# Later norm broadcast, later transposes of branches B and C, later cross-attention scores in a two-layer decoder trunk

## Chip, cores and metric

The kernel runs on one core of one Trainium2 chip. The metric is the time of one execution on the device in microseconds (us), and of several executions the median. "Faster" and "slower" compare the changed kernel with the one before.

## What is computed

Two layers of a causal decoder trunk on 512 tokens of width 1024, in float32. Cut to what matters:

```
xn = rmsnorm(x)
A,B,C,D = four token mixers of xn @ w_in   # dilated attention, retention,
                                           # differential attention, state space scan
m  = sum_i sigmoid(gate_i) * (branch_i @ w_branch_i)
x  = x + m @ w_mix_out
x  = x + cross_attention(rmsnorm(x) @ w_xq, memory of 256 tokens, 4 heads) @ w_xo
x  = x + swiglu(rmsnorm(x) @ w_ffn_in) @ w_ffn_out
```

C works head by head (4) on blocks of 128 queries (qb = 0 to 3): two softmax maps per head, their weighted difference times V, then a norm over each head. B is a retention in blocks of 128 tokens with a state carried from block to block, a norm per head and a gate.

## The kernel before, in words

**Products.** Every float32 operand is held as a pair of rounded parts, hi and lo. One block of weights (128 x 128) against 512 tokens is three matmuls 128x512 (`mm3`, recorded as L266); this text calls the three *one product*. Weights come in chunks of 8 blocks: a transfer (L231), a rounded copy on ACT (L245), the remainder on DVE or POOL (L248), begun three chunks ahead. PSUM has 8 banks in one queue: `bank()` takes the oldest free one, `freebank` puts one back at the end. Each engine works through its instructions in the order in which the program issues them.

**Background items.** The mixers and the cross-attention are Python generators that issue a few instructions and then `yield`. Up to three items are open; each open item moves by one step per two products (`beat` L214, `step`, `go`), and `yield n` makes it sit out until the n-th step from there. So `yield 5` puts ten products between what stands before it and what stands behind it. The four banks that items may hold are counted in `bgbanks`. `finish(prefix)` (L197) runs steps one after another, with no product between them, until the items of that name are done; `finish("C")` stands after the three projections BQK, BV, BG of branch B, whose four results each are copied out by ACT (L424) when the projection's last product is in.

**Items that the change touches.** `c_item`: two score matmuls (L495), mask and maximum on DVE (L500, one per map, then the two banks go back), exp on ACT (L507), normalising on DVE (L510 to L514), transposes on PE (L520), their copy on ACT (L523), the product with V (L531); for the last head of a block also four squares on ACT (L543), an rsqrt on DVE (L544, L328 to L337), the scaling (L546), `yield 5`, four transposes (L554, recorded as L347), and the writes of the result on ACT and DVE (L562, L563). `b_item`: rotation on DVE and POOL (L602 to L608), `yield 5`, transposes (L615), scores (L624, L630, L635), the products with values and state (L646, L648; the state is written at L657 and L659), statistics (L667 to L671, rsqrt), gate (L680, L683, L684), `yield 5`, transposes (L690), and the tail (L581, L585, L586). `x_item` (L1054): scores (L1063), maximum (L1069), exp, transposes (L1090), copies (L1094, L1095), the product with V (L1102), a split into hi and lo (L343, L344).

**Norm.** `fm` (L274) makes a projection with its output features on partitions. Where it has to scale by the norm of its input it starts the products on the unscaled input, issues the statistic behind them (`norm_stat` L381: four small matmuls, an rsqrt on DVE, two diagonal matrices at L399), and leaves the broadcast (`norm_bcast` L405: two matmuls with `onesr`, a copy on ACT at L409) and the scaled evacuations (L418 on DVE) to be issued later:

```
            if norm:
                self.norm_stat()
                self.later = [18, out]
```

`beat` takes 3 from that number per product and calls `out` at zero, so 18 is six products. This happens six times: before `w_in`, `w_xq` and `w_ffn_in` in both layers.

Of the kernel before, what the change touches and what calls it, by code (L numbers as in the profile page):

```python
# [20 lines left out]
NT = T // 128  # L21
# [36 lines left out]
class Prog:  # L58
# [215 lines left out]
    def fm(self, name, l, cols, xs, evac, outer=False, k0=0, norm=None, need=None):  # L274


        K = len(xs)
        if outer:
            bs = [self.bank() for _ in cols]
            for k in range(K):  # L280
                if need:
                    need(k)
                for j, c in enumerate(cols):
                    self.mm3(self.P(bs[j]), self.w(name, l, k0 + k, c), xs[k], k == 0, k == K - 1)

            def out():
                if norm:
                    self.norm_bcast()
                    norm()
                for j, b in enumerate(bs):  # L290
                    evac(j, self.P(b))
                    self.freebank(b)
            if norm:
                self.norm_stat()
                self.later = [18, out]
            else:
                out()
            return
        for j, c in enumerate(cols):
            b = self.bank()  # L300
            for k in range(K):
                self.mm3(self.P(b), self.w(name, l, k0 + k, c), xs[k], k == 0, k == K - 1)
            evac(j, self.P(b))
            self.freebank(b)
# [183 lines left out]
    def c_item(self, h, qb):  # L488
        nc = self.nc
        n = (qb + 1) * 128  # L490
        q, k, v = self.C
        bs = yield from self.bgbanks(2)
        for e in range(2):
            s = slice(64 * e, 64 * e + 64)
            self.mm(self.P(bs[e])[:, :n], self.U(q + h)[s, qb * 128:n], self.U(k + h)[s, :n], True, True)  # L495
        yield 3
        p = yield from self.bu(2)
        mx, den, rd = self.sm(2, "mx"), self.sm(2, "den"), self.sm(2, "rd")
        for e in range(2):
            nc.vector.tensor_tensor_reduce(  # L500
                out=self.U(p[e])[:, :n], in0=self.P(bs[e])[:, :n], in1=self.gc(G_MC + 512 - n, n), scale=1.0,
                scalar=-3e38, op0=OP.add, op1=OP.max, accum_out=mx[:, e:e + 1])
        self.bgfree(*bs)
        nc.vector.tensor_scalar(mx, mx, -0.125, None, op0=OP.mult)
        for e in range(2):
            pe = self.U(p[e])[:, :n]
            nc.scalar.activation(out=pe, in_=pe, func=AF.Exp, scale=0.125, bias=mx[:, e:e + 1],  # L507
                                 accum_out=den[:, e:e + 1])
        yield 6
        nc.vector.reciprocal(out=rd, in_=den)  # L510
        nc.vector.tensor_tensor(out=rd[:, 1:2], in0=rd[:, 1:2], in1=self.nlam, op=OP.mult)
        p0, p1 = self.U(p[0])[:, :n], self.U(p[1])[:, :n]
        nc.vector.tensor_scalar(p0, p0, rd[:, 0:1], None, op0=OP.mult)
        nc.vector.scalar_tensor_tensor(out=p0, in0=p1, scalar=rd[:, 1:2], in1=p0, op0=OP.mult, op1=OP.add)  # L514
        self.release(p[1])
        yield 3
        (b,) = yield from self.bgbanks(1)
        for kb in range(qb + 1):
            s = slice(kb * 128, kb * 128 + 128)
            self.transpose(self.P(b)[:, s], p0[:, s])  # L520
        self.release(p[0])
        pt = yield from self.bu(1)
        nc.scalar.activation(out=self.U(pt)[:, :n], in_=self.P(b)[:, :n], func=AF.Copy)  # L523
        self.bgfree(b)
        yield 2
        yield from self.turn("C", qb * 4 + h)
        if h == 0:
            (self.c_o[qb],) = yield from self.bgbanks(1)
        o = self.P(self.c_o[qb])[:, h * 128:h * 128 + 128]
        for kb in range(qb + 1):  # L530
            self.mm(o, self.U(pt)[:, kb * 128:kb * 128 + 128], self.U(v + kb)[:, h * 128:h * 128 + 128],  # L531
                    kb == 0, kb == qb)
        self.release(pt)
        self.passed("C")
        if h < 3:
            return
        yield 2
        ob = self.P(self.c_o[qb])
        t0 = yield from self.bu(1)
        ss = self.sm(4, "ss")  # L540
        for j in range(4):
            s = slice(j * 128, j * 128 + 128)
            nc.scalar.activation(out=self.U(t0)[:, s], in_=ob[:, s], func=AF.Square, accum_out=ss[:, j:j + 1])  # L543
        nc.vector.tensor_scalar(ss, ss, 1.0 / 128, EPS, op0=OP.mult, op1=OP.add)  # L544
        r = self.rsqrt(ss, 4)
        nc.vector.tensor_tensor(out=self.U(t0).rearrange("p (h e) -> p h e", h=4),  # L546
                                in0=ob.rearrange("p (h e) -> p h e", h=4),
                                in1=r.unsqueeze(2).to_broadcast([128, 4, 128]), op=OP.mult)
        self.bgfree(self.c_o[qb])
        yield 5  # L550
        (b,) = yield from self.bgbanks(1)
        for j in range(4):
            s = slice(j * 128, j * 128 + 128)
            self.transpose(self.P(b)[:, s], self.U(t0)[:, s])  # L554
        self.release(t0)
        yield 1
        yield from self.new_y("C")
        y = self.y["C"]
        s = slice(qb * 128, qb * 128 + 128)
        src = self.P(b).rearrange("p (h e) -> p h e", h=4)  # L560
        hi = self.Q(y[0])[:, :, s]
        nc.scalar.activation(out=hi, in_=src, func=AF.Identity, scale=self.subg)  # L562
        nc.vector.scalar_tensor_tensor(out=self.Q(y[1])[:, :, s], in0=src, scalar=self.subg,  # L563
                                       in1=hi.bitcast(F32), op0=OP.mult, op1=OP.subtract)
        self.bgfree(b)
# [24 lines left out]
    def b_item(self, l, t):  # L590
# [17 lines left out]
        e1.tensor_tensor(out=d[:, :, 1], in0=d[:, :, 1], in1=m[:, 1], op=OP.add)  # L608
        self.release(rot)
        self.release(ta)  # L610
        yield 5
        (b,) = yield from self.bgbanks(1)
        for j in range(4):
            s = slice(j * 128, j * 128 + 128)
# [68 lines left out]
        nc.vector.scalar_tensor_tensor(out=gt, in0=self.U(th), scalar=1.0, in1=gt, op0=OP.add, op1=OP.mult)  # L683
        nc.vector.tensor_tensor(out=self.U(on), in0=self.U(on), in1=gt, op=OP.mult)  # L684
        self.release(th)
        yield 5
        (b,) = yield from self.bgbanks(1)
        for j in range(4):
            s = slice(j * 128, j * 128 + 128)
# [364 lines left out]
    def x_item(self, l, h):  # L1054
        nc = self.nc
        sc = 128 ** -0.5
        KT = self.U(self.KT + h // 2)[:, (h % 2) * MEM:(h % 2) * MEM + MEM]
        q = self.U(self.xq + h)
        bs = yield from self.bgbanks(2)
        for a in range(2):  # L1060
            for e in range(2):
# [472 lines left out]
```

## Time and profile before

| | |
|---|---|
| median of 3 runs | 2304.02 us (2303.53 to 2304.30) |
| the profiled execution, its own time | 2304.3 us |
| its span, first to last instruction | 2302.5 us |
| mean granted TensorE clock | 0.997 |
| busy: PE, DVE, ACT, POOL | 2268.9, 1177.1, 822.6, 612.5 us |
| HBM traffic | 92 GB/s over the span |

The page gives busy time per engine, the span in 40 slices, the DMA queues, the chain of work that ended last, and the costliest groups. PE is TensorE's matmuls, DVE is VectorE, ACT is ScalarE, POOL is GpSimd. A row of the timeline has start, duration, engine, line, operation, output and inputs, and in brackets the idle time of that engine just before and what ended it. Neighbouring instructions of one form are one row (x2, x4).

### The profile page before, as it was taken

To read this page: it belongs to the slowest core of one execution; us is meant where nothing else is said; L and a number is where in the kernel's file an instruction comes from. 1 tells how busy PE (TensorE), PEld (TensorE's weight loads), DVE (VectorE), ACT (ScalarE), POOL (GpSimd) and SP (SyncE) were. 2 spreads that over 40 slices of the span, in tenths; PEclk is the share of its full clock that TensorE was granted. 3 is DMA by queue.
4 is the path that set the end of the run, shared out by engine and by line. 5 is a ranking of instruction groups with operands and counts; after the bars stand their busy time and mean duration, and the time that the engine had idled before them with its cause. 6 is when DMAs were issued, how large, how long until landed. Compare 5 with 4: busy or idle time off the path is not lost.

```text
span 2302.5 us, 27327 instructions
## 1 busy us (share of the span) xinstructions
PE 2268.9 (99%) x10690; PEld 1830.0 (79%) x10690; DVE 1177.1 (51%) x2231; ACT 822.6 (36%) x1408; POOL 612.5 (27%) x300
## 2 busy tenths in 40 slices
PE   8999999999999999999999999999999999999998
PEld 6887777777888778888888877777878877888886
DVE  6865442635846664341347554255575655544312
ACT  5433433343234533232324244334422443332221
POOL 2153222223222122222225322222322222222232
PEclk9999999999999999999999999999999999999999
DMA  6222222222343233333332222222223432233331
GB/s 227 83 65 83 75 72 83 83 66 86 97 129 110 74 100 102 92 100 101 124 99 74 82 74 74 73 83 81 89 62 108 139 100 83 83 101 99 102 101 64
DMA packets 61762, 214.23 MB, mean 93 GB/s; under 512 B 7104, under 2 KB 7488, under 8 KB 61376
## 3 DMA queue, kind: packets, MB, share of 16 engines
q1 hardware_dynamic: 61200, 211.84, 29.4%
q8 instruction: 84, 1.38, 0.2%
q10 hardware_dynamic: 432, 0.64, 0.1%
q14 instruction: 46, 0.38, 0.1%
HBM read 208.26 MB, written 4.19 MB: 92 GB/s over the span
## 4 chain that ended last, share of the span: by engine, by line
PE 70%; DVE 4%; ACT 1%; issue 0%; ACTq 0%
PE ps L266 69%; PE ps L347 1%; DVE u L683 0%; DVE u L680 0%; DVE rq_z L337 0%; DVE bst L667 0%; DVE rq_a L334 0%; DVE rq_a L335 0%; DVE u L684 0%; DVE lo L248 0%; DVE u L659 0%; DVE rq_i L328 0%; DVE u L926 0%; DVE q L586 0%; DVE u L928 0%
## 5 line engine op out<-in xcount | busy, mean ns | idle before, releaser
L266 PE MATMUL ps<-u,hi 128*128 128x512 f32 x3936 | 1229.7, 393 | 1.2 <-ACT u L343 0.7
L248 POOL TENSOR_TENSOR lo<-raw,hi 128x1024 fp32r<-128x1024 f32 x213 | 519.5, 2440 | 1654.1 <-ACT hi L245 1609.3
L266 PEld LDWEIGHTS ps<-u,hi 128*128 128x128 f32 x3936 | 728.8, 188 | 161.5 <-issue 10.5
L266 PE MATMUL ps<-u,lo 128*128 128x512 f32 x1968 | 767.5, 390 | 0.0
L245 ACT ACTIVATE hi<-raw 128x1024 fp32r<-128x1024 f32 x372 | 389.4, 1051 | 338.0 <-PE ps L266 229.0
L266 PEld LDWEIGHTS ps<-u,lo 128*128 128x128 f32 x1968 | 369.4, 188 | 78.4
L248 DVE TENSOR_TENSOR lo<-raw,hi 128x1024 fp32r<-128x1024 f32 x159 | 205.3, 1293 | 346.6 <-ACT hi L245 345.9
L266 PE MATMUL ps<-hi,u 128*128 128x512 f32 x1120 | 355.3, 398 | 0.4 <-DVE u L973 0.4
L266 PEld LDWEIGHTS ps<-hi,u 128*128 128x128 f32 x1120 | 206.5, 189 | 52.4 <-issue 11.2
L266 PE MATMUL ps<-lo,u 128*128 128x512 f32 x560 | 219.8, 393 | 4.0 <-DVE lo L248 4.0
L266 PE MATMUL ps<-q,hi 128*128 128x512 f32 x640 | 201.4, 396 | 0.0
L266 PE MATMUL ps<-u 128*64 128x128 f32 (+8 forms) x1218 | 175.4, 341 | 7.5 <-ACT u L1000 3.2
L266 PEld LDWEIGHTS ps<-u 128*128 128x128 f32 (+2 forms) x1218 | 120.3, 174 | 51.1 <-issue 27.9
L266 PEld LDWEIGHTS ps<-q,hi 128*128 128x128 f32 x640 | 117.3, 188 | 29.0 <-issue 5.2
L266 PEld LDWEIGHTS ps<-lo,u 128*128 128x128 f32 x560 | 105.8, 189 | 27.4 <-DVE lo L248 4.6
L266 PE MATMUL ps<-q,lo 128*128 128x512 f32 x320 | 124.9, 390 | 0.0
L917 ACT ACTIVATE u<-u 128x512 f32<-128x512 f32 x64 | 40.4, 632 | 211.3 <-DVE u L916 200.3
L916 DVE TENSOR_TENSOR u<-ps,u 128x512 f32<-128x512 f32 x64 | 44.0, 688 | 121.8 <-PE ps L266 121.8
L347 PE MATMUL ps<-gcst,u 128*128 128x128 f32 x448 | 70.7, 274 | 6.3 <-DVE u L684 3.3
L1125 DVE TENSOR_TENSOR u<-ps,u 128x512 f32<-128x512 f32 x44 | 30.4, 691 | 90.1 <-PE ps L266 89.4
L347 PEld LDWEIGHTS ps<-gcst,u 128*128 128x128 f32 x448 | 55.2, 140 | 24.4 <-DVE u L684 4.6
L266 PEld LDWEIGHTS ps<-q,lo 128*128 128x128 f32 x320 | 60.1, 188 | 13.0
(225 smaller groups left out, 1706.8 us busy)
## 6 DMA issues: line engine op xcount, KB each, us to landing
raw<-wall SPq DMA_DIRECT2D x372, 512.0 KB, 3.6
q<-memt SPq DMA_DIRECT2D x6, 512.0 KB, 6.5
q<-xt SPq DMA_DIRECT2D x2, 1024.0 KB, 8.3
u<-rot SPq DMA_DIRECT2D x8, 256.0 KB, 4.0
u<-xt SPq DMA_DIRECT2D x8, 256.0 KB, 6.1
xd<-u SPq DMA_DIRECT2D x8, 256.0 KB, 2.0
u<-xd SPq DMA_DIRECT2D x8, 256.0 KB, 5.1
out<-u SPq DMA_DIRECT2D x6, 256.0 KB, 2.5
```

The lines of the kernel that those rows point to most:

```text
L245: nc.scalar.activation(out=h, in_=r, func=AF.Copy)
L248: eng.tensor_tensor(out=lo, in0=r, in1=h.bitcast(F32), op=OP.subtract)
L266: self.nc.tensor.matmul(out, lhsT=a, rhs=b, start=start, stop=stop)
L347: self.nc.tensor.transpose(out, src, self.ident)
L916: nc.vector.tensor_tensor(out=self.U(u), in0=ps, in1=self.U(self.rb), op=OP.mult)
L917: nc.scalar.activation(out=self.U(u), in_=self.U(u), func=AF.Tanh, scale=0.5)
L1125: nc.vector.tensor_tensor(out=self.U(t), in0=ps, in1=self.U(self.rb), op=OP.mult)
```

## The change

Five numbers change; nothing is computed differently.

```diff
@@ fm (L295)
-                self.later = [18, out]
+                self.later = [24, out]
@@ c_item, ahead of the transposes of a block's result (L550)
-        yield 5
+        yield 6 if qb < NT - 1 else 5
@@ b_item, ahead of the transposes L615
-        yield 5
+        yield 8
@@ b_item, ahead of the transposes L690
-        yield 5
+        yield 8
@@ x_item, ahead of the scores L1063
+        yield 1
         bs = yield from self.bgbanks(2)
```

Since each item moves by steps and at most three are open, an item that ends later also lets the next one start later. What that does to the order in which instructions stand is shown at three places. Names carry the program's buffer numbers where rows would read alike.

**ACT at the end of branch C in layer 0** (L424 are the copies of the projection BG, L543 the squares of the last head, L562 the write of the last block). Before:

```order
L523 ACTIVATE u<-ps 128x512 x2
L245 ACTIVATE hi<-raw 128x1024
L543 ACTIVATE u,ss<-ps 128x128 x4
L424 ACTIVATE u<-ps,rth 128x512 x4
L562 ACTIVATE q<-ps,subg 128x4x128
```

After the change:

```order
L523 ACTIVATE u<-ps 128x512
L245 ACTIVATE hi<-raw 128x1024
L523 ACTIVATE u<-ps 128x512
L424 ACTIVATE u<-ps,rth 128x512 x4
L543 ACTIVATE u,ss<-ps 128x128 x4
L562 ACTIVATE q<-ps,subg 128x4x128
```

The squares stand in front of BG's four copies before, behind them now.

**Scores of block 3, head 0 of branch C in layer 0**, on PE (the matmuls 128x128 with `u_2732` to `u_2734` are a product with V, `u_2513,u_1602 128x512 x2` the two score matmuls, the rest products). Before:

```order
L266 MATMUL ps_89<-lo_3499,u_99 128x512
L266 MATMUL ps_89<-u_2732,u_3702 128x128
L266 MATMUL ps_89<-u_2733,u_3702 128x128
L266 MATMUL ps_89<-u_2734,u_3702 128x128
L266 MATMUL ps_89<-u_2513,u_1602 128x512 x2
L266 MATMUL ps_89<-hi_3497,u_99 128x512
L266 MATMUL ps_89<-hi_3497,u_107 128x512
L266 MATMUL ps_89<-lo_3499,u_99 128x512
```

After the change:

```order
L266 MATMUL ps_89<-lo_3499,u_99 128x512
L266 MATMUL ps_89<-u_2732,u_3700 128x128
L266 MATMUL ps_89<-u_2733,u_3700 128x128
L266 MATMUL ps_89<-u_2734,u_3700 128x128
L266 MATMUL ps_89<-hi_3497,u_99 128x512
L266 MATMUL ps_89<-hi_3497,u_107 128x512
L266 MATMUL ps_89<-lo_3499,u_99 128x512
L266 MATMUL ps_89<-hi_3555,u_100 128x512
L266 MATMUL ps_89<-hi_3555,u_108 128x512
L266 MATMUL ps_89<-lo_3557,u_100 128x512
L266 MATMUL ps_89<-u_2513,u_1602 128x512 x2
```

The two score matmuls stand two products later, one product behind the first use of a new chunk (`hi_3555`). On DVE at the same place (`u_3719` or `u_3735` are the scores of block 2, head 3). Before:

```order
L563 SCALAR_TENSOR_TENSOR q_3401<-ps_89,subg_432,q_3400 128x4x128
L500 ISA u_3719,mx_3721<-ps_89,gcst_90 128x384
L500 ISA mx_3721 128x1
L500 ISA u_3720,mx_3721<-ps_89,gcst_90 128x384
L500 ISA mx_3721 128x1
L504 TENSOR_SCALAR mx_3721<-mx_3721 128x2
L248 TENSOR_TENSOR lo_3738<-raw_3632,hi_3736 128x1024
```

After the change:

```order
L563 SCALAR_TENSOR_TENSOR q_3407<-ps_89,subg_432,q_3406 128x4x128
L248 TENSOR_TENSOR lo_3726<-raw_3632,hi_3724 128x1024
L510 RECIPROCAL rd_3661<-den_3660 128x2
L511 TENSOR_TENSOR rd_3661<-rd_3661,nlam_440 128x1
L513 TENSOR_SCALAR u_3657<-u_3657,rd_3661 128x384
L514 SCALAR_TENSOR_TENSOR u_3657<-u_3658,rd_3661,u_3657 128x384
L500 ISA u_3735,mx_3737<-ps_89,gcst_90 128x384
L500 ISA mx_3737 128x1
L500 ISA u_3736,mx_3737<-ps_89,gcst_90 128x384
```

The maxima of block 2, head 3, stand in front of the chunk's remainder (L248) before, behind it and behind the normalising of another head now. The second score matmul of block 3, head 0, writes the bank that the first of these two maxima gives back.

**The norm broadcast of the feed-forward part of layer 1**, on PE (`onesr` is the broadcast, L347 transposes of the layer's input). Before:

```order
L266 MATMUL ps_89<-u_14601,onesr_93 128x512
L266 MATMUL ps_89<-u_14602,onesr_93 128x512
L347 MATMUL ps_89<-gcst_90,u_13538 128x128
L347 MATMUL ps_89<-gcst_90,u_13539 128x128
L347 MATMUL ps_89<-gcst_90,u_13540 128x128
L347 MATMUL ps_89<-gcst_90,u_13541 128x128
L266 MATMUL ps_89<-u_100,hi_14465 128x512
```

After the change:

```order
L347 MATMUL ps_89<-gcst_90,u_13538 128x128
L347 MATMUL ps_89<-gcst_90,u_13539 128x128
L347 MATMUL ps_89<-gcst_90,u_13540 128x128
L347 MATMUL ps_89<-gcst_90,u_13541 128x128
L266 MATMUL ps_89<-u_100,hi_14465 128x512
L266 MATMUL ps_89<-u_108,hi_14465 128x512
L266 MATMUL ps_89<-u_100,lo_14467 128x512
L266 MATMUL ps_89<-u_101,hi_14465 128x512
L266 MATMUL ps_89<-u_109,hi_14465 128x512
L266 MATMUL ps_89<-u_101,lo_14467 128x512
L266 MATMUL ps_89<-u_14601,onesr_93 128x512
L266 MATMUL ps_89<-u_14602,onesr_93 128x512
```

The broadcast stands two products and the four transposes later.

`finish("C")` runs 7 steps in layer 0 (6 before) and 6 in layer 1 (5 before). Between the last head's product with V and the last transposes L554 stand three products in layer 0 (five before) and four in layer 1 (six before). In layer 1 the squares stay in front of BG's copies.

## Rows read from the trace of the kernel before

**Rows 1.** The page: busy time, and the chain that ended last.

```profile
PE 2268.9 (99%) x10690; PEld 1830.0 (79%) x10690; DVE 1177.1 (51%) x2231; ACT 822.6 (36%) x1408; POOL 612.5 (27%) x300
...
PE 70%; DVE 4%; ACT 1%; issue 0%; ACTq 0%
```

**Rows 2.** Waits of PE: who waits, for whom, us in total, times, longest.

```profile
PE ps L347 <- DVE u L684: 3.3, 3, 1.4
...
PE ps L266 <- DVE u L399: 2.8, 2, 1.4
PE ps L266 <- DVE u L418: 2.1, 2, 1.4
PE ps L347 <- DVE u L608: 1.7, 1, 1.7
...
PE ps L266 <- DVE u L659: 0.9, 1, 0.9
...
PE ps L266 <- ACT u L343: 0.7, 1, 0.7
PE ps L266 <- ACT u L523: 0.7, 1, 0.7
```

**Rows 3.** Windows, branch B, layer 0: length, busy of PE, PEld, DVE, ACT, POOL; clock.

```profile
560.00:602.00 42.00, 40.16 (x211) 33.08 (x210) 37.38 (x110) 11.45 (x16) 9.21 (x5) 1.00 0.19 59
```

**Rows 4.** Timeline at the end of branch C, layer 0: PE, ACT and DVE.

```profile
530.24 0.39 PE L266 MATMUL ps<-lo,u 128*128 128x512 f32 x1
...
530.92 0.39 PE L266 MATMUL ps<-lo,u 128*128 128x512 f32 x1
532.32 0.63 PE L347 MATMUL ps<-gcst,u 128*128 128x128 f32 x4 [1.01 <-DVE u L546]
...
527.93 0.28 ACT L543 ACTIVATE u<-ps 128x128 f32<-128x128 f32 x1 [2.07 <-PE ps L266]
...
529.31 2.73 ACT L424 ACTIVATE u<-ps,rth 128x512 f32<-128x512 f32 x4 [0.24 <-PE ps L266]
...
529.10 0.17 DVE L544 TENSOR_SCALAR ss<-ss 128x4 f32<-128x4 f32 x1 [1.98 <-ACT u L543]
```

**Rows 5.** Timeline of PE around the norm broadcasts of the feed-forward part, both layers.

```profile
828.76 1.10 PE L266 MATMUL ps<-u,onesr 128*128 128x512 f32 x2 [1.36 <-DVE u L399]
829.70 0.62 PE L266 MATMUL ps<-u,hi 128*128 128x512 f32 x2
...
1955.30 1.01 PE L266 MATMUL ps<-u,onesr 128*128 128x512 f32 x2 [1.39 <-DVE u L399]
1956.14 0.60 PE L347 MATMUL ps<-gcst,u 128*128 128x128 f32 x4
1956.50 0.71 PE L266 MATMUL ps<-u,hi 128*128 128x512 f32 x2
```

**Rows 6.** Timeline of PE at the end of branch C, layer 1.

```profile
1653.79 0.63 PE L347 MATMUL ps<-gcst,u 128*128 128x128 f32 x4 [0.34 <-DVE u L546]
```

**Rows 7.** Timeline of ACT and DVE around the scores of block 3, head 0, layer 0.

```profile
469.28 1.06 ACT L245 ACTIVATE hi<-raw 128x1024 fp32r<-128x1024 f32 x1 [3.40 <-issue]
...
471.52 0.16 DVE L510 RECIPROCAL rd<-den 128x2 f32<-128x2 f32 x1
...
472.77 0.16 DVE L510 RECIPROCAL rd<-den 128x2 f32<-128x2 f32 x1
...
463.24 0.55 DVE L500 CUSTOM_DVE_ANT_0 u<-ps,gcst 128x384 f32<-128x384 f32 x1
```

**Rows 8.** PE's longest idle time, and windows with the granted clock (the number after POOL's).

```profile
15.51 0.79 PE L266 MATMUL ps<-lo,u 128*128 128x512 f32 x1 [3.98 <-DVE lo L248]
...
14.00:14.50 0.50, 0.00 (x0) 0.00 (x0) 0.50 (x1) 0.29 (x1) 0.42 (x2) 0.51 0.00 0
...
20.50:21.00 0.50, 0.50 (x3) 0.40 (x2) 0.50 (x1) 0.00 (x0) 0.42 (x2) 0.66 1.21 475
...
2291.95 0.39 PE L266 MATMUL ps<-lo,u 128*128 128x512 f32 x1
...
2297.50:2298.00 0.50, 0.00 (x0) 0.00 (x0) 0.22 (x1) 0.12 (x1) 0.00 (x0) 0.53 0.00 0
```

## Prediction

> **What bounds the kernel now.** I read the page first: PE is busy 99% of the span and PE's own lines make up 70% of the chain that ended last; DVE is busy half of the time [rows 1]. The change removes no work from PE, so only the time in which PE stands still can change. Next I read PE's waits [rows 2]: they are short (the longest outside the start is 1.7 us), and nearly all are for a result of DVE. The windows tell what kind of wait it is: in branch B of layer 0 DVE is busy 37.4 of 42 us [rows 3], so there DVE is the limit for a while and PE runs into it at single places. The timelines then give the price of each place. A product is three matmuls and takes 530.92 - 530.24 = 0.68 us [rows 4], so each matmul follows the last after 0.23 us. A wait that is listed with 1.01 us delays the transposes behind it by 532.32 - 530.92 - 0.23 = 1.17 us [rows 4]: I add 0.16 us to each listed idle time.
>
> **What the change takes away.**
>
> *Branch B.* PE waits for L684 three times, for L608 once and for L659 once: 3.3 + 1.7 + 0.9 = 5.9 us listed [rows 2], with 5 x 0.16 us it is 6.7 us. Two of these are in layer 0, three in layer 1. Both transposes come three steps later, that is six products or 6 x 0.68 = 4.1 us, and the second gets both delays. The longest of these waits is 1.7 us, so each is covered twice over, unless DVE's backlog moves with it. DVE had 4.6 us to spare in the 42 us [rows 3], and the work that the items hand it is the same, only later. I take the whole 6.7; the bounds are 0 and 6.7.
>
> *Norm broadcast.* Two of the six places wait, both at the feed-forward part, for L399 [rows 2, 5]. In layer 0 the first `onesr` starts 1.36 + 0.16 us late, and the pair takes 829.70 - 828.76 = 0.94 us instead of 0.46, as its second half waits for the second diagonal: some 2.0 us in all. Two products more cover 1.36 of it. In layer 1 the lateness is 1.39 + 0.16 us and the pair takes 1956.14 - 1955.30 = 0.84, in all 1.9 us, and the four transposes (0.36 us from start to the next product) now stand in front too: 1.36 + 0.36 = 1.72. Together 3.1.
>
> *Scores of the cross-attention.* They wait for L418 in both layers, 2.1 us with the longest 1.4 [rows 2], so 0.7 + 0.16 and 1.4 + 0.16. One step later is two products, 1.36 us: all of the first and 1.36 of the second, 2.2 us.
>
> Sum of the gains: 6.7 + 3.1 + 2.2 = 12.0 us. The other four norm broadcasts show no wait; there the later start only keeps two to four banks 1.36 us longer, which I cost at nothing because the projections behind have other banks.
>
> **What it adds.** All of it is in branch C and the cross-attention, where `finish` and the queues of ACT and DVE decide.
>
> *End of C, layer 0.* The item's last step comes one step later, so `finish` meets the transposes with three products behind the last product with V instead of five. The squares now stand behind BG's four copies on ACT, and the fourth copy needs BG's very last product. From rows: that product's last matmul ends at 530.92 + 0.39 = 531.31, the four copies at 529.31 + 2.73 = 532.04, 0.73 later. The squares take 529.10 - 527.93 = 1.17, and from L544 to the transposes it is 532.32 - 529.10 = 3.22 [rows 4]. So the transposes start 0.73 + 1.17 + 3.22 = 5.1 us after the last product ends, 5.5 after its last matmul started, where 0.23 would be undisturbed: PE stands 5.3 us instead of 1.17. **Cost 4.1.** No other work can cover it, as `finish` issues none.
>
> *End of C, layer 1.* The squares keep their place; two products fewer stand in front of the transposes, and PE already waits there (0.34 us [rows 6]). Cost 1.36.
>
> *Scores of block 3, head 0, layer 0.* They now come one product behind the first use of a new chunk, and their second bank is given back by a maximum that stands behind that chunk's remainder on DVE. ACT starts the rounded copy when the chunk changes (469.28); normalising starts 471.52 - 469.28 = 2.24 us later, takes 472.77 - 471.52 = 1.25, the maximum 0.55 [rows 7]: 4.04 us after the change of chunk. PE is there after one product and one score matmul, 0.94 us. Cost 3.1.
>
> *Smaller ones.* The order shows three more places in C where a bank is taken whose copy or maximum was issued just before, and two in the cross-attention where a product follows the split behind more work of ACT. No row shows them. The nearest are a wait for such a copy (L523) and for such a split (L343), each 0.7 + 0.16 us [rows 2]; each place costs between 0 and 0.9. I take 0.55 for the three (1.7 in all) and half, 0.43, for the two (0.9): 2.6, with 0 and 4.3 as bounds.
>
> Sum of the costs: 4.1 + 1.4 + 3.1 + 2.6 = 11.2 us. **Gains less costs: 0.8 us faster.** The profiled execution took 2304.3 us (span 2302.5 and 1.8 around it), so 2303.5; the median is 0.3 below that execution, so I forecast **2303.2 us**.
>
> **The rivals.**
>
> *The clock falls at the end of C.* PE stood 3.98 us at the start, and the granted clock was at its lower level from 14.0 to about 20.8 us; after its last matmul (2291.95 + 0.39) it fell about 5.2 us later [rows 8]. A stop of 5.3 us in layer 0 lies between these cases. At the start PE worked from 15.5 to 20.8 at 1.2 in place of 2.4 GHz, which cost half of 5.3 us, some 2.7 us. Against it: none of the stops of up to 1.7 us lowered the clock, and at the start PE had been running unevenly before. The Trainium skill (TensorE: Matmul & The Clock Gate, "Why this matters for your kernels") advises against idle gaps between bursts of matmuls, because the array then goes back to half speed; the start of this trace agrees. Time: 2303.2 + 2.7 = 2305.9 us, still within 0.2%.
>
> *The new waits of C and the cross-attention are hidden.* If the banks come free earlier than the queues let me think (a chunk's copy ahead of its place, another bank at the head of the queue), 3.1 + 2.6 = 5.7 us are not paid. Then 2297.5 us, faster. For it: before, PE waits only once each for L523 and L343 in some 2300 us. Against it: the order of DVE's queue is fixed and the rows give its length.
>
> *DVE's backlog moves with branch B* (slower). Items that sit out longer hand DVE the same work in a shorter rest of the stage, and L684 comes later by as much as the transposes. Then PE's waits for L684, L608 and L659 stay, and 6.7 us are not gained: 2309.9. It is slower by over 0.2% where more than 5.4 of the 6.7 stay. For it: DVE is busy 89% there. Against it: the lateness would have to reach 4 to 8 us.
>
> *The change does nothing*: the steps move but neither the waits nor the queues. 2304.0. The order speaks against it.
>
> **How the numbers follow.** A measurement of this kernel tells 0.2%, 4.6 us, from no change: faster is below 2299.4, slower above 2308.6. Forecast 0.38, its own range 2299 to 2307 by the bounds of the smaller costs and of the norm broadcasts. Clock 0.27, hidden waits 0.18, B's waits stay 0.12, nothing 0.05. Faster: 0.18 and 0.05 of the forecast's lower end, 0.23. Slower: 0.12 and 0.05 of the clock case with a smaller gain in B, 0.17. The rest, 0.60, is within 0.2%. Range 2297 to 2309: it takes in the hidden waits and the clock, and leaves out B's waits and the ends of the others.
>
> **What would show it.** In the profile after: no wait of PE for L684, L608 and L659; a wait for L399 of at most 0.6 us; a wait for L418 of at most 0.3; one wait for L546 of about 5 us near 530 and one of about 1.7 near 1653; a wait of about 3 us for L500 near 468. The granted clock between 530 and 545 tells the clock case. It is wrong if the waits of B remain (then the backlog was the cause, not the place of the transposes), if the wait at the end of C in layer 0 is under 3 us, or if PE waits for a line that is not named here.

## The result and the profile after

| | before | after |
|---|---|---|
| median of 6 runs | 2303.96 us (2303.53 to 2304.30) | 2319.84 us (2317.36 to 2322.18) |
| profiled execution, its span | 2304.3, 2302.5 us | 2317.36, 2315.6 us |
| mean granted clock in it | 0.997 | 0.995 |

The ratio is 1.0068, with a 95% interval of 1.0057 to 1.0078: **15.9 us slower**, where 2303.2 us and "no change" were forecast. The profiled execution is the fastest of the six, so the trace accounts for 13.1 of these 15.9 us; the other five had a clock of 0.993 or so and spread up to 2322.18.

The page after (busy time, then the chain that ended last) answers to [rows 1]:

```profile
PE 2276.7 (98%) x10690; PEld 1834.5 (79%) x10690; DVE 1190.1 (51%) x2231; ACT 822.9 (36%) x1408; POOL 610.5 (26%) x300
...
PE 74%; DVE 5%; ACT 1%; issue 1%; ACTq 0%
```

The work is the same (10690 matmuls), yet PE is busy 7.8 us longer: some of its matmuls ran slower, or no longer beside another. The rest of the longer span is idle time. PE's waits after (for whom, us in total, times, longest), to be held against [rows 2]:

```profile
PE ps L347 <- DVE u L546: 6.7, 2, 5.0
PE ps L266 <- ACT u L617: 4.3, 1, 4.3
...
PE ps L347 <- DVE u L684: 2.3, 1, 2.3
PE ps L266 <- DVE mx L500: 2.2, 1, 2.2
PE ps L266 <- DVE q L563: 1.5, 1, 1.5
...
PE ps L347 <- DVE u L1085: 0.7, 1, 0.7
```

L399, L418, L608 and L659 are gone, as forecast, and L546 and L500 have come, as forecast. L617, L563 and L1085 were named nowhere as waits, and L684 is one wait of 2.3 us in place of three of up to 1.4 us. The windows with the granted clock (after POOL's busy time) show three stretches at the lower of its two levels, 1.2 instead of 2.4 GHz, that the kernel before has nowhere but at its start and end:

```profile
472.70:476.10 3.40, 3.40 (x9) 2.75 (x9) 2.18 (x9) 0.91 (x4) 0.00 (x0) 0.50 0.03 7
541.00:547.80 6.80, 5.19 (x15) 4.25 (x16) 4.67 (x9) 1.63 (x2) 2.36 (x1) 0.50 0.00 0
629.70:633.10 3.40, 3.40 (x14) 2.69 (x15) 2.07 (x5) 0.82 (x1) 2.50 (x1) 0.50 0.07 28
```

Each begins behind or within a stop of PE: that for L500, L546 and L617. PE worked 3.40, 5.19 and 3.40 us at half speed in them, and half of that is lost: 1.7 + 2.6 + 1.7 = 6.0 us.

Where the two traces part is read from the start of the same matmul, by its count, after less before, at the borders of the stages:

| stage | forecast, us | measured, us |
|---|---|---|
| branch C, layer 0 | +7.2, and some of the 1.7 of smaller places | +13.7 |
| branch B, layer 0 | -2.2 | +3.8 |
| cross-attention, layer 0 | -0.4 | +1.3 |
| norm broadcast of the feed-forward part, layer 0 | -1.4 | -1.4 |
| branch C, layer 1 | +1.4, and the rest of the 1.7 | +2.2 |
| branch B, layer 1 | -4.5 | -2.4 |
| cross-attention and norm broadcast, layer 1 | -2.6 | -3.1 |
| everything else | 0 | -1.0 |

Two stages carry most of the miss: **C and B of layer 0**. The 1.0 us of the last row were gained ahead of branch C: at the start the clock was at its lower level for 3.4 us (15.3 to 18.7) in this execution and for 6.8 us (14.0 to 20.8) in the one before.

PE in C, layer 0, after (start, duration, line, operation; idle time and what ended it in brackets):

```profile
468.32 1.12 PE L266 MATMUL ps<-u 64*128 64x512 f32 x2
471.64 1.12 PE L266 MATMUL ps<-u 64*128 64x512 f32 x2 [2.20 <-DVE mx L500]
472.70 0.80 PE L266 MATMUL ps<-hi,u 128*128 128x512 f32 x1
...
508.90 1.12 PE L266 MATMUL ps<-u 64*128 64x512 f32 x2
511.49 1.12 PE L266 MATMUL ps<-u 64*128 64x512 f32 x2 [1.47 <-DVE q L563]
512.54 0.73 PE L266 MATMUL ps<-hi,u 128*128 128x512 f32 x2
...
537.22 0.39 PE L266 MATMUL ps<-lo,u 128*128 128x512 f32 x1
542.61 1.08 PE L347 MATMUL ps<-gcst,u 128*128 128x128 f32 x4 [5.01 <-DVE u L546]
```

At the end of C PE stands 542.61 - 537.22 - 0.23 = 5.16 us; 5.3 were forecast. The scores of block 3, head 0, take 472.70 - 468.32 = 4.38 us. How long they take undisturbed is shown by the next such scores before the change:

```profile
503.85 1.13 PE L266 MATMUL ps<-u 64*128 64x512 f32 x4 [0.69 <-ACT u L523]
504.91 0.50 PE L266 MATMUL ps<-hi,u 128*128 128x512 f32 x1
```

Each of the two score matmuls of a head is recorded as two rows (x2). Issued together, all four rows take 504.91 - 503.85 = 1.06 us; after the change each pair of rows takes that long by itself (472.70 - 471.64 = 1.06). A wait between the two score matmuls of a head so costs its idle time and 1.06 us for the overlap that is lost: 4.38 - 1.06 = 3.3 us at this place, with 3.1 forecast.

What stops PE in B, layer 0, after: first PE, then ACT, then DVE.

```profile
624.95 0.39 PE L266 MATMUL ps<-u,lo 128*128 128x512 f32 x1
629.63 1.18 PE L266 MATMUL ps<-u 64*128 64x128 f32 x8 [4.29 <-ACT u L617]
...
623.36 1.05 ACT L245 ACTIVATE hi<-raw 128x1024 fp32r<-128x1024 f32 x1
628.46 0.63 ACT L585 ACTIVATE q<-u 128x512 fp32r<-128x512 f32 x1 [4.05 <-DVE u L581]
628.99 0.58 ACT L617 ACTIVATE u<-ps 128x512 f32<-128x512 f32 x1
...
624.43 2.06 DVE L248 TENSOR_TENSOR lo<-raw,hi 128x1024 fp32r<-128x1024 f32 x1 [2.52 <-ACT hi L245]
626.42 0.68 DVE L926 SCALAR_TENSOR_TENSOR u<-u,ps 128x512 f32<-128x512 f32 x1
627.13 0.69 DVE L928 TENSOR_TENSOR u<-u 128x512 f32<-128x512 f32 x1
627.74 0.68 DVE L581 TENSOR_TENSOR u<-ps,vec 128x512 f32<-128x512 f32 x1
```

Read it backwards. The last block's scores need its transposes, which L617 copies out of PSUM. On ACT that copy stands behind L585, the tail of the block before, and ACT sits idle for 4.05 us because L585 needs L581 on DVE. DVE has L581 behind a chunk's remainder (L248), L926 and L928. So PE waits 4.3 us, through ACT, for an instruction that stands late in DVE's order. DVE was not overloaded there: it had sat idle for 2.52 us until ACT had made the rounded copy for L248. Before the change, L617 of the last block stood 7.6 us ahead of that L585 on ACT:

```profile
598.76 0.58 ACT L617 ACTIVATE u<-ps 128x512 f32<-128x512 f32 x1
...
606.40 0.61 ACT L585 ACTIVATE q<-u 128x512 fp32r<-128x512 f32 x1
```

### The profile page after: what moved, and what is told of

Its sections match the earlier page's. It is cut to its first block, busy times and chain, and to the rows that moved or that the text cites. A ratio compares the mean times of both kernels' runs of the same rounds, so it can differ in the third digit from the quotient of the medians.

```text
span 2315.6 us, 27319 instructions
## 1 busy us (share of the span) xinstructions
PE 2276.7 (98%) x10690; PEld 1834.5 (79%) x10690; DVE 1190.1 (51%) x2231; ACT 822.9 (36%) x1408; POOL 610.5 (26%) x300
## 4 chain that ended last, share of the span: by engine, by line
PE 74%; DVE 5%; ACT 1%; issue 1%; ACTq 0%
PE ps L266 72%; PE ps L347 2%; DVE lo L248 0%; DVE rq_a L335 0%; DVE u L1085 0%; DVE u L680 0%; DVE rq_a L334 0%; DVE rq_i L328 0%; ACT hi L245 0%; DVE u L926 0%; DVE rq_z L337 0%; DVE bst L667 0%; DVE u L916 0%; DVE rq_y L330 0%; DVE u L683 0%
## 5 line engine op out<-in xcount | busy, mean ns | idle before, releaser
L248 POOL TENSOR_TENSOR lo<-raw,hi 128x1024 fp32r<-128x1024 f32 x213 | 518.7, 2436 | 1672.1 <-ACT hi L245 1567.5
L248 DVE TENSOR_TENSOR lo<-raw,hi 128x1024 fp32r<-128x1024 f32 x159 | 205.3, 1293 | 339.6 <-ACT hi L245 339.1
L347 PE MATMUL ps<-gcst,u 128*128 128x128 f32 x448 | 71.9, 276 | 9.7 <-DVE u L546 6.7
L347 PEld LDWEIGHTS ps<-gcst,u 128*128 128x128 f32 x448 | 55.6, 141 | 28.2 <-issue 7.5
```

The source lines that it names most:

```text
L248: eng.tensor_tensor(out=lo, in0=r, in1=h.bitcast(F32), op=OP.subtract)
L347: self.nc.tensor.transpose(out, src, self.ident)
```

## Experiments

Theory A: branch C's moved transposes carry the loss, as new waits and through the clock that falls behind them. Rival B: it is the backlog of branch B. Rival C: the parts harm only together. Each kernel is an edit of the kernel before or of the changed one, and each was timed against the kernel before (medians 2303.76 to 2303.90 us).

### The four parts one by one

```diff
-                self.later = [18, out]
+                self.later = [24, out]
```

> Only the norm broadcast is moved (24 in place of 18); C, B and the cross-attention keep their numbers. Theory (the loss sits in C and B and in the clock that falls behind their stops): the two waits for L399 (2.8 us listed) go as in the profile of the change, about 3 us faster, 2301 us. Rival (the later broadcast keeps banks longer and pushes the projections behind it): no gain or slower, 2304 us or more.

2303.50 us, ratio 0.9998 (0.9989 to 1.0007): no difference. The waits for L399 are gone, but the cross-attention of layer 0 has a new one, for normalised scores (L1084). It stands within the first head's transposes. First PE, then DVE, then POOL:

```profile
PE ps L347 <- DVE u L1084: 1.3, 1, 1.3
...
758.49 0.38 PE L347 MATMUL ps<-gcst,u 128*128 128x128 f32 x2
760.18 1.03 PE L347 MATMUL ps<-gcst,u 128*128 128x128 f32 x6 [1.31 <-DVE u L1084]
...
757.13 3.25 DVE L1084 TENSOR_SCALAR u<-u,rd 128x256 f32<-128x256 f32 x4
...
757.61 2.37 POOL L248 TENSOR_TENSOR lo<-raw,hi 128x1024 fp32r<-128x1024 f32 x1 [11.36 <-ACT hi L245]
```

The four operations L1084 of a head usually take 1.14 us; here one of them takes 2.46 us by itself, from 757.66 to 760.12, while POOL works on a chunk's remainder until 759.98. PE waits for that one. Besides, the last head's transposes have no product behind them in `finish` (one before the change), which costs 0.4 us. A miss for the theory; its rival had the time nearly right, but not the place.

```diff
         q = self.U(self.xq + h)
+        yield 1
         bs = yield from self.bgbanks(2)
```

> Only the scores of the cross-attention come one step later. Theory: the two waits for L418 (2.1 us listed) go, a wait for L1085 of some 0.7 us comes in layer 0: 1 to 1.5 us faster, about 2302.7 us. Rival (the finish of the cross-attention takes back all of it, as it runs one step more without products): 2304 us or more.

2304.20 us, ratio 1.0001 (0.9993 to 1.0010). The same picture: L418 is gone, and 1.3 us for L1085 have come in its place, in the same transposes and again behind one operation of 2.46 us beside POOL's L248; the missing product in `finish` costs 0.9 us here. L399 stays with 2.8.

```diff
-        yield 5
+        yield 6 if qb < NT - 1 else 5
```

(in `c_item`)

> Only the transposes of branch C are a step later (blocks 0 to 2). Theory: the waits of C in the profile of the change come alone: 3.3 us at the scores of block 3, head 0, about 2 at the scores that wait for L563, 4.1 at the end in layer 0, 2 in layer 1, some 11 us, and 0 to 5 us more where the clock falls behind a stop: 2315 to 2320 us. Rival (most of the loss comes from B): 2304 to 2308 us.

2320.15 us, ratio 1.0074 (1.0061 to 1.0086): this one number alone makes the kernel slower by 16.3 us, as much as the whole change. The waits for L546 (6.7 us, longest 5.0), L500 (2.2) and L563 (1.5) are there, and the clock is at 0.50 in 473.1 to 476.5 and 541.4 to 548.2. Theory A stands.

```diff
-        yield 5
+        yield 8
...
-        yield 5
+        yield 8
```

(both in `b_item`)

> Only branch B's two transposes are three steps later. Theory: the five waits of before (some 7 us) go, a wait of 4.4 us for L617 in layer 0 and one of 2.4 for L684 in layer 1 come in their place, and the clock may fall behind the first (0 to 3 us): 2303 to 2307 us. Rival 1 (as the prediction had it): 2297 us. Rival 2 (B carries most of the loss): 2312 us or more.

2306.39 us, ratio 1.0010 (1.0001 to 1.0019), so 2.5 us slower where the prediction has 6.7 faster. L608 and L659 are gone, and two waits have come that are as large, with the clock at its lower level behind the first:

```profile
PE ps L266 <- ACT u L617: 4.0, 1, 4.0
...
PE ps L347 <- DVE u L684: 2.2, 1, 2.2
```

```profile
616.00:622.60 6.60, 6.38 (x20) 5.06 (x21) 2.36 (x5) 1.11 (x2) 2.77 (x1) 0.50 0.32 95
```

### The norm broadcast and the cross-attention together

> The later norm broadcast and the later scores of the cross-attention together, B and C as before. Alone they gave 2303.5 and 2304.2, as in each a wait for L1084 or L1085 of 1.3 us came in place of the one removed in layer 0. Theory (together the two steps keep their distance): both the waits for L399 and L418 go and 0.7 us remains: 2300.5 to 2301.5 us. Rival (the gain is given back again): 2303.5 us or more.

Both edits from above: 2300.64 us, ratio 0.9986 (0.9977 to 0.9995). Neither is worth anything alone, together they save 3.2 us: each by itself brings the first head's normalising beside an operation of POOL, and PE waits 1.3 us; with both it is the third head's, and PE waits 0.7 us. With this the parts add up: 16.3 + 2.5 - 3.2 = 15.6 of the 15.9 us. Rival C falls for C and B; it holds only for this pair.

### Is the clock a cost of its own?

The changed kernel, with matmuls whose results are overwritten put ahead of the stops at L546 (layer 0) and L617, so that PE is busy until what it waits for is there:

```diff
         (b,) = yield from self.bgbanks(1)
+        if qb == NT - 1 and not hasattr(self, "fill_c"):
+            self.fill_c = True
+            for _ in range(20):
+                self.mm(self.P(b), self.onesr, self.UR(self.hh), True, True)
...
         sb = yield from self.bgbanks(3 if t < NT - 1 else 2)
+        if t == NT - 1 and l == 0:
+            for _ in range(16):
+                self.mm(self.P(sb[0]), self.onesr, self.UR(self.hh), True, True)
```

> The changed kernel, with matmuls that serve nothing put into PE's two longest stops: 20 of 128x512 in front of the last transposes of C in layer 0 (4.5 us into a stop of 5.2), 16 in front of the last block's scores of B in layer 0 (3.6 us into one of 4.4). The waits themselves stay as long as they are. Theory (a stop lowers the clock, and the half level behind it costs 1.7 to 2.6 us each): the granted clock stays up at both places and the time falls by 3.4 to 5.2 us, from 2319.8 to about 2315.5 us. Rival (only the waits count, the clock follows from something else): same as the changed kernel, 2319.8, or slower by the added work.

2315.33 us: 4.5 us *less* than the changed kernel, with 36 matmuls more; the slowest of these runs (2316.86) is faster than the fastest of the changed kernel (2317.36). The windows show why, at the end of C (first two) and behind L617 (third), while the last shows a fall behind the stop of 1.5 us at L563, which the profiled execution after does not have:

```profile
538.00:545.00 7.00, 6.51 (x30) 5.10 (x28) 2.67 (x13) 3.08 (x11) 0.00 (x0) 1.00 0.34 126
545.00:552.00 7.00, 7.00 (x33) 5.89 (x34) 5.44 (x6) 1.74 (x3) 4.64 (x4) 1.00 0.13 23
630.00:634.00 4.00, 4.00 (x19) 3.27 (x19) 1.80 (x4) 0.01 (x1) 2.80 (x1) 1.00 0.06 12
514.30:517.60 3.30, 3.30 (x9) 2.55 (x9) 2.87 (x9) 1.52 (x4) 0.00 (x0) 0.50 0.04 17
```

The stops are as long as before to within 0.3 us, PE only fills them. Held against the profiled execution after, matmul by matmul, this one gains 2.4 us at the end of C and 2.0 behind L617, and loses 1.6 behind L563. So the 4.3 us (2.6 + 1.7) that the two slow stretches were reckoned at are the clock's, and not part of the waits.

### What makes the two waits in C

The squares of the last block one step earlier, beside the edit of C:

```diff
         if h < 3:
             return
-        yield 2
+        yield 2 if qb < NT - 1 else 1
```

> The later transposes of C alone (2320.15 us), with the squares of the last block one step earlier, so that ACT has them in front of BG's four copies again in layer 0; the number of products between stays three. Theory (order on ACT): the stop at the end of C in layer 0 falls from 5.2 to about 2.6 us, 2317.6, and 2315 if the clock then stays up. Rival (the missing two products alone make the stop): still 5 us, 2320.

2316.14 us, ratio 1.0052 (1.0040 to 1.0065), 4.0 less than C alone. The longest wait for L546 falls from 5.0 to 2.4 us, and the clock stays up:

```profile
540.00:546.00 6.00, 5.22 (x25) 4.43 (x26) 4.46 (x5) 1.64 (x2) 2.84 (x2) 1.00 0.00 0
```

So the place of the squares on ACT, behind BG's four copies, makes 2.6 us of this stop and, in the profiled execution, the fall of the clock behind it. The 2.4 us that stay are the 1.0 of before [rows 4] and the 1.36 of the two missing products.

The remainders of the two chunks that stand in front of the scores' maxima on POOL instead of DVE, beside the edit of C:

```diff
-        eng = nc.gpsimd if i > 16 and i % 5 in self.pool_lo else nc.vector
+        eng = nc.gpsimd if i > 16 and (i % 5 in self.pool_lo or i in (74, 79)) else nc.vector
```

> The later transposes of C alone (2320.15 us), with the remainders of chunks 74 and 79 on POOL instead of DVE. Theory (the second score matmul waits for a maximum that stands behind the chunk's remainder and the normalising on DVE): the stop of 2.2 us at the scores of block 3, head 0 goes, with the lost overlap of the two score pairs and the half-level clock behind it, some 5 us; the one behind L563 shrinks by 0.6: 2314 to 2315 us. Rival (the bank is late for another reason): 2320.

2314.61 us, ratio 1.0045 (1.0032 to 1.0057), 5.5 less than C alone. The wait for L500 is gone, and what is left at the second place is

```profile
PE ps L266 <- DVE q L563: 0.9, 1, 0.9
```

The clock falls once, behind L546. The chunk's remainder on DVE was the cause: 3.3 us for the first place, 1.7 for the clock behind it and 0.6 at the second are 5.6.

### What makes the wait in B, and a better kernel

The tail's rounding copy on DVE, so that ACT has nothing in front of L617 that waits for DVE; with both numbers of B at 8:

```diff
-        nc.scalar.activation(out=hi, in_=tmp, func=AF.Copy)
+        nc.vector.tensor_copy(hi, tmp)
```

> The later transposes of B alone (2306.4 us), with the rounded copy in the tail (L585) on DVE instead of ACT, in B and D. DVE waits 0.7 us for that copy now and would take about as long for it itself. Theory (the copy L617 is done long before PE wants it, but stands behind L585 on ACT, which waits for L581 on DVE): the stop of 4.1 us for L617 in layer 0 goes, and the half-level clock behind it: 2306.4 less 4 to 6.5 us, 2300 to 2302.5. Rival (L617 is late because the transposes or its bank are): 2306.

2298.90 us, ratio 0.9979 (0.9970 to 0.9988): 7.5 less than B alone, more than was expected, as in B alone the slow stretch behind L617 lasted 6.6 us and not 3.4 as after the whole change: the stop of 4.0 + 0.16 us and half of the 6.38 us that PE worked in the stretch add up to 7.4. ACT and DVE there:

```profile
609.21 1.04 ACT L245 ACTIVATE hi<-raw 128x1024 fp32r<-128x1024 f32 x1
610.15 0.57 ACT L617 ACTIVATE u<-ps 128x512 f32<-128x512 f32 x1
...
615.07 0.68 DVE L581 TENSOR_TENSOR u<-ps,vec 128x512 f32<-128x512 f32 x1
615.78 0.43 DVE L585 CAST q<-u 128x512 fp32r<-128x512 f32 x1
```

L617 runs right behind a chunk's copy, no wait for it is left, and PE's clock stays up. The copy costs DVE 0.43 us, less than the 0.70 us for which DVE sat idle for ACT's copy in each tail; so DVE is not charged more by it (in the last run below one such copy, beside POOL, takes 1.96 us). D's tails have the copy on DVE too. By its trace this run gains on B alone at the place of L617 and a little at L684, and nowhere else; the copy without the edits of B was not run.

The rest of the change without its edit of C, and with that copy on DVE:

> The change without its edit to branch C, with the tail's rounded copy on DVE. Theory (the parts add up): 2300.6 of the two norm and cross-attention edits, less 2.2 of B in layer 0 and 2.4 in layer 1: 2296 us. Rival (B's gain is given back at another place once the stop for L617 is gone): 2300 us or more.

2295.82 us, ratio 0.9966 (0.9953 to 0.9978). The only wait of B that is left is 1.9 us for L684 in layer 1. One step more in front of the transposes L690 (`yield 9`):

> As the last, with nine steps in place of eight in front of B's second transposes. Theory (the wait of 2.3 us for L684 in layer 1 is the only one of B that is left, and one step is 1.36 us): 1.4 us less than the last, 2294.7. Rival (the next item comes later with it and the wait moves): the same as the last or slower.

**2293.70 us** (2293.15 to 2293.89), ratio 0.9956 (0.9943 to 0.9968): 10 us faster than the kernel before, 26 faster than the changed one, with no wait of B left: 2.1 less than the last, where 1.4 were expected.

The same with fewer steps, 6 in front of L615 and 7 in front of L690:

> As the last two, with six and seven steps in front of B's transposes. Theory (DVE's backlog in B lasts about two steps, so most of the gain needs no more): 2296 to 2298 us. Rival (fewer steps leave the waits of before): 2300 us.

2305.68 us, ratio 1.0008 (1.0000 to 1.0017), a miss by far. Both last blocks' transposes now wait for L608:

```profile
PE ps L347 <- DVE u L608: 7.7, 2, 4.7
```

DVE in layer 1 there:

```profile
1728.50 1.22 DVE L248 TENSOR_TENSOR lo<-raw,hi 128x1024 fp32r<-128x1024 f32 x1
1729.64 1.36 DVE L680 TENSOR_SCALAR u<-ps,bmv,rq_z 128x128 f32<-128x128 f32 x4
...
1731.63 0.69 DVE L684 TENSOR_TENSOR u<-u 128x512 f32<-128x512 f32 x1
...
1732.57 0.42 DVE L608 TENSOR_TENSOR u<-u 128x256 f32<-128x256 f32 x1
```

The rotation of the last block (L607, L608) has come to stand behind a remainder and another block's whole gate (L680 to L684). In the profiled execution, one of the slowest with 2307.67 us, the clock fell behind both stops. More steps are not simply better and fewer not simply worse: a number decides which item's work stands in front of which on DVE and ACT.

## Why the prediction was wrong, step by step

**Right: the large costs in C.** The stop at the end of C was forecast at 5.3 us in layer 0 and is 5.16; in layer 1 at 0.5 + 1.36 = 1.86, and it is listed with 1.7, so 1.86. The scores of block 3, head 0, cost 3.3 with 3.1 forecast. Their causes are shown by moving the squares and the remainder. The method, the order of ACT's and DVE's queues with durations from rows, found these places and their causes. At the scores luck helped the size: a wait of about 3 us for L500 was named, and it is listed with 2.2, as the first score matmul by itself takes 1.06 us and not the 0.26 (0.94 - 0.68) that the prediction gave it; the lost overlap makes up for the shorter wait.

**Wrong: that B's waits are "covered twice over" (6.7 us).** All the old ones went as argued, but the step asked only whether the *same* wait could come later. Later items also put other work in front: a tail's copy ahead of L617 on ACT in layer 0 (4.29 + 0.16 us), and in layer 1 two tails and half a rotation ahead of the gate (2.3 + 0.16). These give back 6.9 us, and the clock behind L617 costs 1.7 more. In layer 1 a second cause stands beside this order and was not told apart from it: three operations of the rsqrt ahead of that gate ran beside POOL and took 3.2 us longer than usual (last section). The rival "DVE's backlog moves with branch B" had this price, 6.7 us, but not this place: it asked for waits for L684, L608 and L659, and only L684 is among them. It got 0.12 on the ground that the lateness "would have to reach 4 to 8 us"; the order of ACT's queue at L617 would have shown otherwise, and it was not read. What B is worth without the wait for L617 is shown with the tail's copy on DVE: 4.9 us faster with both numbers at 8.

**Wrong: the clock as a rival of its own with one fall.** The text reckoned 2.7 us for one fall at the end of C; that fall cost 2.6. But the clock was tied to the longest stop alone, and it fell at three places, 6.0 us in the profiled execution; its argument, "none of the stops of up to 1.7 us lowered the clock", left the range from 1.7 to 5 us open and the stops of 2.2 to 4.3 us went uncounted. The clock should have been in the sum of every stop above what the trace had shown to be free. The Trainium skill (TensorE: Matmul & The Clock Gate, "Why this matters for your kernels") says the same in general, that idle gaps between bursts of matmuls send the array back to half speed; this trace agrees, with 0.50 behind stops of 2.2, 4.3 and 5.0 us.

**Mis-sized: the smaller places in C.** 0.55 each for three. The scores behind L563 cost 512.54 - 508.90 - 1.06 = 2.6 us, against 0.85 for the wait for L523 that stood there before: 1.7 more, for this place alone. Its idle time of 1.5 us is above the bound of 0.9 that was taken from other kinds of wait, and the lost overlap of the two pairs was in no row that was read.

**Mis-sized: the cross-attention of layer 0.** Its scores no longer wait (0.9 us gained), but the forecast 0.4 for smaller places is 2.2. L1085 takes 0.7 and 0.16, as two operations of the third head's normalising ran beside POOL and took 2.49 and 2.47 us instead of 0.35; the last transposes in `finish` take the rest:

```profile
799.53 1.55 PE L347 MATMUL ps<-gcst,u 128*128 128x128 f32 x8
801.33 1.98 PE L266 MATMUL ps<-u 128*128 128x512 f32 x4 [0.25 <-ACT u L1095]
```

From the transposes to the products with V it is 1.80 us. Eight such transposes of the heads before take 0.8 us to the next product; the item ends later, and `finish` runs its last steps with nothing to cover them. That is the trap that was reckoned for C and not for this item.

**Right: the norm broadcasts.** 1.36 us gained in layer 0, as worked out, and layer 1 with its cross-attention gained 3.1 for 2.6.

In sum, over the profiled execution: 0.8 us were to be gained and 13.1 were lost, 13.9 apart. The clock makes 6.0 of that, B without it 6.9, the second place in C 1.1 and the cross-attention of layer 0 1.7: 15.7. From it go 0.5 for the cross-attention of layer 1 and 1.0 for the start; in B the single sums are 0.5 above what the borders of the stages show, and this was not followed further. That the other executions take 2.5 us more than the profiled one was not traced: the lower mean clock of 0.993 points to further falls, like that behind L563, but this is argued and not shown.

## What to carry to other kernels

Work that is moved back along a fixed order does not only meet its own inputs later: at every engine it passes, look for what now stands in front of its next step, above all an instruction that itself waits for another engine. Price a stop of the matmul engine at its idle time plus the slow stretch behind it, unless the trace shows stops of that length to be free. A stage's last item has no cover in `finish`, and to leave its own number alone does not protect it: in C the last block kept its 5, yet it came a step later, as the items in front of it ended later. A shift by a few products can also bring operations of two engines side by side that ran apart before; look for single operations that have become longer.

## What the runs showed that was not expected

- The clock fell behind stops that are listed with 2.2 us (L500) and once with 1.5 (L563, in the run with filled stops), and did not behind one of 2.4 us (the squares moved), nor behind the same 1.5 us in the profiled execution after. Idle time alone did not decide it. The slow stretch lasted about 3.4 us in some executions and 6.8 in others, also behind one and the same stop (L617: 3.4 after the whole change, at least the 6.6 of the window shown in B alone), so one fall cost between 1.7 and 3.2 us.
- Two score matmuls of 64 rows each, issued one behind the other on the two halves of the partitions, share PE: both together (four rows) took 1.06 us, and one alone (two rows) took 1.06 as well. The Trainium skill (TensorE: Matmul & The Clock Gate, "Why this matters for your kernels") states that matmuls with few rows run concurrently when each lies in its own group of rows; the trace agrees, and adds that a wait between them takes it away.
- Single small operations of DVE take many times their usual time, and each time POOL is at work. In the profiled execution after, 102 of DVE's 2231 operations took over 0.5 us longer than the median of their line and form. All 102 overlap an operation of POOL, and only 379 of the 2231 do so at all; in the execution before it is 95 of 95. One stands in front of the late gate in B, layer 1, and ends when POOL's operation does:

```profile
1734.32 2.37 DVE L334 SCALAR_TENSOR_TENSOR rq_a<-rq_y,bvar 128x4 f32<-128x4 f32 x1
...
1734.28 2.39 POOL L248 TENSOR_TENSOR lo<-raw,hi 128x1024 fp32r<-128x1024 f32 x1 [18.29 <-ACT hi L245]
```

The next two operations of the rsqrt, beside POOL's L603 and L605, take 0.67 and 0.66 us instead of 0.16. The remainder L248 ahead of L581 in B, layer 0, took 2.06 us in place of 1.22, also beside POOL. The traces show the overlap; no run took POOL's operation away to test it.
